# Layer 0 of a two-layer trunk: the matmuls of each small job ranked 40 places ahead, as a group

## The chip, the cores and the metric

The kernel runs on one core of a Trainium2 chip. The metric is the device time of one execution in microseconds, and the median over runs is compared.

## The reference, cut to what matters

The reference computes a trunk of two layers on 512 tokens of width 1024, in fp32. Layer 0 mixes tokens with two recurrences side by side, HGRN2 (4 heads of 128) and RWKV7 (8 heads of 64). Layer 1 does block attention. Each layer has an MLP and a gated side input behind its mixer.

```
def hgrn_rwkv_mixer(h, w_in, w_out, ...):
    u = h @ w_in
    hq, hf, hi, hg, ur = split(u)
    o_a = hgrn2_chunked(silu(hq), 1 - f, hi, log(f))     # f from hf
    o_a = rms_norm(o_a) * silu(hg)
    r, k, v, wd, ad, gd = split(ur + (token_shift(ur) - ur) * mu)
    y = rwkv7_scan(r, decay, k, v, kk, a)                # state per head, token by token
    o_b = (head_layer_norm(y) + bonus) * g
    return concat([o_a, o_b]) @ w_out

for l in range(2):
    x = x + mixer[l](rms_norm(x))
    x = x + square(relu(rms_norm(x) @ w_up[l])) @ w_down[l]
    x = x + rms_norm(p[l] @ ple_proj[l]) * sigmoid(x @ ple_gate[l])
```

## The kernel before

**Large products.** Every product with a weight matrix goes through `gemm`. It splits weights and activations into a high and a low fp32r part and calls `mm3` (L243), three passes of 128x512 for each 128x128 block of weights (L244 whi times high, L245 whi times low, L246 wlo times high). A pass has a weight load of its own. Weights come in halves of 128x512: a DMA on SyncE (L231), a cast on ScalarE (L236, `whi`), a subtraction on VectorE (L237, `wlo`). In layer 0 two raw halves and three split ones are kept. Below, "large pass" means L244 to L246.

**Small jobs.** The recurrences are rewritten in chunks, and their matmuls are small: 64 to 256 columns, most in plain fp32 (two records each in the trace), those of the triangular inverse (L519, L664) in fp16 (one record). Some write only half of the array's columns (L631, L726, L731; the trace has them as 128\*64). They come in groups of three to eight that fill one PSUM tile, and one VectorE or ScalarE instruction then takes the tile away. In the trace the group of `half4` is L664, that of `four` is L519.

**Stages of layer 0.** For each of four heads `step` runs the letters of `ORDER = "AFHBOC"`:
- A: `p2(h, 0)`, the inverse (L519, then L664 level after level, L676 to L690), woven with the side jobs `p3(h-1, 1)` (L707 to L754: states), `p1(h, 1)` (L600 to L631) and `tail(h-1)`.
- F: the three large products f, q, i of the HGRN head (`proj_h`).
- H: `hgrn` (transposes L803, L831, five levels L851, L868 to L884, output transposes L896); its g product is asked for inside.
- B: `proj_rkv(h+1)`, three large products r, k, v of the next RWKV head pair.
- O: `out_piece(h-1)`, the output product of the head before. After the last head `out_piece(3)`.
- C: `p2(h, 1)` woven with `pre(h+1)` and `p3(h, 0)`, then `p1(h+1, 0)`.

**What sets the order.** All instructions are traced in program order; then a planner deals them out. On every engine it takes, among the instructions whose inputs and buffers are ready in its own model of time, the one with the lowest rank. The order on each engine is fixed by this before the chip runs. An instruction's rank is a counter that goes up by one with each traced instruction. `tc.high_priority(offset)` sets the counter back by `offset` at its start, and puts it at its end to where it was at its start. So the instructions inside take no ranks away from what follows, and two such blocks in a row begin at the same rank.

`run` (steps A and C) and the products of step B use an offset of 300:

```
    def run(*gens):
        with tc.high_priority(offset=OFS):
            for g_ in gens:
                for _ in g_:
                    pass
...
                with tc.high_priority(offset=OFS if h else 0):
                    proj(WI[nm, h], evac)
```

The ranks that follow, for the first heads: step A of head 0 has -47 to 105, F and H of head 0 have 253 to 498. Then B (the products r, k and v of head 1) has 199 to 231 three times, step C of head 0 has 199 to 400 with its p1 at 199 to 243, and step A of head 1 has 199 to 427. F and H of head 1 follow with 499 to 744, B for head 2 with 445 to 477, O with 745 to 812, C of head 1 with 513 to 714, and so on. So the large passes of B, and the instructions of C and of the next A, have equal ranks over a good part of their length. Behind the mixer all ranks go up in program order.

PSUM has eight tiles: two for `pj` (large products), two for `pmh` (HGRN and norms), four for `pmr` (RWKV, and the first large products).

Of the kernel before, what the change touches and what calls it, by code (L numbers as in the profile page):

```python
# [34 lines left out]
OFS = 300  # L35
NWARM = 9

P = 128
S = 512
D = 1024  # L40
NJ = S // P
# [144 lines left out]
def trunk(ctx, tc, wts, xT, pT, vecs, lora, cst, lev, seg, rope, gain, out, upto="all", dbg=None, mode=None):  # L186
    nc = tc.nc
    V, A, G, T = nc.vector, nc.scalar, nc.gpsimd, nc.tensor
# [20 lines left out]
    ident = cc("ident")  # L209
# [32 lines left out]

    def mm3(ps, wh, wl, xh, xl, first, last):  # L243
        T.matmul(ps, wh, xh, start=first, stop=False)  # L244
        T.matmul(ps, wh, xl, start=False, stop=False)  # L245
        T.matmul(ps, wl, xh, start=False, stop=last)  # L246
# [37 lines left out]
    class Stats:  # L284
# [4 lines left out]
        def add(self, sq, rhs):  # L289
            for j in range(NJ):  # L290
                T.matmul(self.ps[:, j * self.cols:(j + 1) * self.cols], sq[:, j * P:(j + 1) * P], rhs,
                         start=(self.i == 0 and j == 0), stop=(self.i == self.n - 1),
                         skip_group_check=True)
            self.i += 1
# [31 lines left out]
    def bcast_rows(rt, cols, pool, tag):  # L326
        ps = pool.tile([P, S], F32, name=tag)
        if cols > 1:
            full = nrm.tile([P, S], F32, name="bc")
            V.tensor_copy(full.rearrange("p (c w) -> p c w", w=P // cols),  # L330
                          rt[:, :, None].to_broadcast([P, NJ * cols, P // cols]))
        for j in range(NJ):
            lhs = full[:, j * P:(j + 1) * P] if cols > 1 else rt[:, j:j + 1].to_broadcast([P, P])
            T.transpose(ps[:, j * P:(j + 1) * P], lhs, ident)
        return ps
# [28 lines left out]
    def layer0_mixer(actp):  # L364
# [151 lines left out]
        def four(lhs, rhs):  # L516
            ps = pmr.tile([P, S], F32, name="pmr")
            for i in range(4):
                T.matmul(ps[:, i * P:i * P + P], lhs(i), rhs(i), start=True, stop=True)  # L519
            return ps.rearrange("p (i t) -> p i t", i=4)  # L520
# [67 lines left out]
        def p1(hp, g):  # L588
            lw, bh, kh, ar, rh_, bo, dl, v, y = pre_[hp]
            gs = slice(g * 256, g * 256 + 256)  # L590
            NA, KA, TOK = NAs[g], KAs, []
            un[hp, g] = (NA, TOK)

            for n, (src, dst) in enumerate(((bh, NA), (kh, KA))):
                for h in range(2):
                    A.copy(BH[hs[h], n, :, hs[h]], src[hs[h], gs].rearrange("p (c t) -> p c t", t=64))
                ps = pmr.tile([P, S], F32, name="pmr")
                for c_ in range(4):
                    o = g * 256 + c_ * 64
                    T.matmul(ps[:, c_ * P:c_ * P + P].rearrange("p (x t) -> p x t", x=2), BH[:, n, c_, :],  # L600
                             ar[:, :, o:o + 64], start=True, stop=True)
                pv = ps.rearrange("p (a c x t) -> p a c x t", a=2, c=2, x=2)
                for h in range(2):
                    for c_ in range(2):
                        V.tensor_tensor(dst[hs[c_], :, h, :, hs[c_]], pv[hs[h], :, c_, :, :],
                                        tri[hs[h], None, :, :].to_broadcast([64, 2, 2, 64]), op=OP.mult)
                yield
            for a in range(2):
                j = 2 * g + a
                js = slice(j * P, j * P + P)  # L610

                ps = pmr.tile([P, S], F32, name="pmr")
                for n, src in enumerate((ar[:, 0, :], v, bh, kh)):
                    T.transpose(ps[:, n * P:n * P + P], src[:, js], ident)
                t = E("TOK", 4, [P, 3, P])
                pv = ps.rearrange("p (x f) -> p x f", x=4)
                A.copy(t[:, 0:2, :], pv[:, 0:2, :])
                for c_ in range(2):
                    A.copy(BZ[g][hs[c_], a, :, c_, :], pv[hs[c_], 2:4, :])
                TOK.append(t)  # L620
                yield

            ps = pmr.tile([P, S], F32, name="pmr")
            for i, (a, h) in enumerate(pk):
                T.matmul(ps[:, i * 64:i * 64 + 64], KA[:, a, h, 0, :], TOK[a][:, 1, hs[h]], start=True, stop=True)
# [4 lines left out]
            for i, (a, h) in enumerate(pk):  # L630
                T.matmul(ps[hs[h], a * P:a * P + P], TOK[a][:, 1, hs[h]], KA[:, a, h, 1, :], start=True, stop=True)  # L631
            A.copy(y[:, gs], ps[:, :256])
            yield

        def p2(hp, g):
# [11 lines left out]
            for l in range(1, 6):  # L647
# [12 lines left out]
                def half4(lhs, rhs):  # L660
                    ps = pmr.tile([P, S], F32, name="pmr")
                    pv = ps[:, :256].rearrange("p (i n u) -> p i n u", i=4, u=H)
                    for i in range(4):
                        T.matmul(pv[:, i], lhs[:, i, :], rhs[:, i], start=True, stop=True)  # L664
                    return pv
# [9 lines left out]
            for i, (a, h) in enumerate(pk):  # L675
                T.matmul(ps[:, i * P:i * P + P], NA[:, a, h, 0, :], tt[:, i, :], start=True, stop=False)  # L676
                T.matmul(ps[:, i * P:i * P + P], id16, id16, start=False, stop=True)
# [4 lines left out]
            for i in range(4):  # L682
                T.matmul(ps[:, i * P:i * P + P], er[:, i, :], XT[:, i, :], start=True, stop=False)
                T.matmul(ps[:, i * P:i * P + P], id16, XT[:, i, :], start=False, stop=True)
# [4 lines left out]
            for i, (a, h) in enumerate(pk):  # L689
                T.matmul(ps[:, i * P:i * P + P].rearrange("p (x f) -> p x f", x=2), tt[:, i, :],  # L690
                         TOK[a][:, 0::2, hs[h]], start=True, stop=True)
# [6 lines left out]
        def p3(hp, g):  # L698
# [5 lines left out]
            for a in range(2):  # L704
# [18 lines left out]
            def inner():  # L723
                ps = pmr.tile([P, S], F32, name="pmr")
                for i, (a, h) in enumerate(pk):
                    T.matmul(ps[hs[h], a * P:a * P + P], MU[:, a, 0, hs[h]], NA[:, a, h, 1, :], start=True, stop=True)  # L726
# [3 lines left out]
                for i, (a, h) in enumerate(pk):  # L730
# [21 lines left out]
            for c_ in range(f, 4):  # L752
                ch = 4 * g + c_
                T.matmul(ps[:, c_ * 64:c_ * 64 + 64], SB[:, ch, :], rh_[:, ch * 64:ch * 64 + 64], start=True, stop=True)  # L754
# [43 lines left out]
        def hgrn(h, q, ff, iv, gproj):  # L798
# [3 lines left out]
            for j in range(NJ):  # L802
                T.transpose(ps[:, j * P:j * P + P], iv[:, j * P:j * P + P], ident)  # L803
# [25 lines left out]
            for j in range(NJ):  # L829
                js = slice(j * P, j * P + P)  # L830
                T.matmul(ps[:, js], ks[:, js], d[:, js], start=True, stop=True)  # L831
            V.copy_predicated(at, m8[:, 13, None, :].to_broadcast([P, NJ, P]), j4(ps))
            for l in range(2, 7):
# [15 lines left out]
                for j in range(NJ):  # L849
                    js = slice(j * P, j * P + P)  # L850
                    T.matmul(ps[:, j * 64:j * 64 + 64], ks[:, js], qs[:, j * 64:j * 64 + 64], start=True, stop=True)  # L851
# [15 lines left out]
            for j in range(3):  # L867
                T.transpose(ps[:, j * P:j * P + P], d[:, j * P:j * P + P], ident)  # L868
# [3 lines left out]
            for j in range(3):  # L872
                T.matmul(ps[:, j * P:j * P + P], kt[:, j * P:j * P + P], vt[:, j, :], start=True, stop=True)
# [6 lines left out]
            for j in range(NJ):  # L880
                js = slice(j * P, j * P + P)
                T.matmul(ps[:, js], at[:, j, :], vt[:, j, :], start=True, stop=(j == 0))
                if j:
                    T.matmul(ps[:, js], q[:, js], st_[:, j * P - P:j * P], start=False, stop=True)  # L884
# [10 lines left out]
            for j in range(NJ):  # L895
                T.transpose(ps[:, j * P:j * P + P], ot[:, j * P:j * P + P], ident)  # L896
# [18 lines left out]
        t = {}  # L915
# [431 lines left out]
```

## Time and profile before

| | |
|---|---|
| median of 3 runs | 1511.21 us (1510.91 to 1512.28) |
| the profiled execution | 1511.89 us, span 1510.1 us |
| mean granted TensorE clock | 0.997 |
| TensorE, matmuls | 1478.1 us busy, 98% |
| TensorE, weight loads (overlap the matmuls) | 1191.3 us, 79% |
| VectorE | 937.6 us, 62% |
| ScalarE | 663.1 us, 44% |
| GpSimd | 138.4 us, 9% |
| the mixer of layer 0 | 0 to 454 us |

The start of a matmul is recorded, its end is modelled, and neighbours overlap in the records: a pass of 128x512 shows some 0.39 us although the next one starts 0.23 us later. What a pass costs is therefore read from start to start. The profile's rows merge instructions of one line that follow each other; a count (x4) tells how many records they are.

### The profile page before, as it was taken

The page shows a single profiled execution, that of the slowest core. Times are in us where ns is not written, and L with a number is a line of the kernel's source. Part 1 is how long each engine was busy: PE and PEld are TensorE (multiplying, and loading weights), DVE is VectorE, ACT ScalarE, POOL GpSimd, SP SyncE. Part 2 cuts the span into 40 slices and gives each one's busy share as a digit, 9 for nine tenths or more (in the row PEclk, how much of TensorE's full clock was granted, in tenths as well). Part 3 has the DMA queues.
Part 4 walks back from the last instruction along what each step waited for, and adds up shares of the span by engine and source line. Part 5 has one row for each costly group of instructions (what it writes and reads, how often), then busy time and mean ns, then how long its engine had stood idle before and what let it go on. Part 6 is the DMA issues. An engine that isn't in the chain of part 4 may idle for free.

```text
span 1510.1 us, 20495 instructions
## 1 busy us (share of the span) xinstructions
PE 1478.1 (98%) x7546; PEld 1191.3 (79%) x7546; DVE 937.6 (62%) x1835; ACT 663.1 (44%) x1269; POOL 138.4 (9%) x133
## 2 busy tenths in 40 slices
PE   8899999999989999999999999999999999999998
PEld 6678777777667888888888888777778888888887
DVE  6878797687785664444446648377575444445463
ACT  4675545554446433333334534455634333333342
POOL 4121220310205000000000200000220000000000
PEclk9999999999999999999999999999999999999999
DMA  5110111211123233333333432221123333333331
GB/s 179 56 36 22 55 50 39 66 29 47 39 91 106 90 98 98 98 98 98 98 95 98 124 118 84 77 63 50 56 80 95 95 101 98 98 96 93 98 98 70
DMA packets 67109, 123.88 MB, mean 82 GB/s; under 512 B 7632, under 2 KB 8016, under 8 KB 67008
## 3 DMA queue, kind: packets, MB, share of 16 engines
q1 hardware_dynamic: 65376, 118.57, 25.6%
q10 hardware_dynamic: 1152, 2.43, 0.5%
q0 software_dynamic: 480, 1.57, 0.3%
q8 instruction: 59, 0.97, 0.3%
q14 instruction: 42, 0.34, 0.1%
HBM read 120.45 MB, written 2.10 MB: 81 GB/s over the span
## 4 chain that ended last, share of the span: by engine, by line
PE 87%; DVE 7%; ACT 3%; issue 2%; DMA 1%; POOL 1%; SPq 0%; DVEq 0%; ACTq 0%; POOLq 0%
PE pj L244 20%; PE pj L246 20%; PE pj L245 20%; PE pmr L1273 1%; PE pmr L245 1%; PE pmr L1249 1%; PE pmr L246 1%; PE pmr L244 1%; PE pj L1176 1%; PE pmr L1176 1%; PE pj L1178 1%; PE pmr L1177 1%; PE pmr L1178 1%; PE pj L1177 1%; PE pmh L1176 1%
## 5 line engine op out<-in xcount | busy, mean ns | idle before, releaser
L236 ACT CAST whi<-wr 128x512 fp32r<-128x512 f32 x428 | 265.0, 621 | 549.2 <-PE pj L245 421.9
L237 DVE TENSOR_TENSOR wlo<-wr,whi 128x512 fp32r<-128x512 f32 x428 | 312.5, 733 | 197.6 <-ACT whi L236 193.6
L244 PE MATMUL pj<-act,whi 128*128 128x512 f32 (+1 forms) x856 | 338.1, 396 | 1.2 <-DVE h L935 1.0
L245 PE MATMUL pj<-act,whi 128*128 128x512 f32 (+1 forms) x856 | 336.8, 394 | 0.0
L246 PE MATMUL pj<-act,wlo 128*128 128x512 f32 (+1 forms) x856 | 335.7, 393 | 0.5 <-DVE wlo L237 0.5
L244 PE MATMUL pj<-hid,whi 128*128 128x512 f32 x512 | 199.2, 389 | 0.0
L245 PE MATMUL pj<-hid,whi 128*128 128x512 f32 x512 | 199.2, 389 | 0.0
L246 PE MATMUL pj<-hid,wlo 128*128 128x512 f32 x512 | 199.2, 389 | 0.0
L244 PEld LDWEIGHTS pj<-act,whi 128*128 128x128 f32 x856 | 161.1, 188 | 34.4 <-ACT k L491 1.4
L246 PEld LDWEIGHTS pj<-act,wlo 128*128 128x128 f32 x856 | 161.2, 188 | 32.5 <-DVE wlo L237 1.5
L245 PEld LDWEIGHTS pj<-act,whi 128*128 128x128 f32 x856 | 161.2, 188 | 31.1 <-issue 1.5
L1115 DVE TENSOR_TENSOR x<-x,pj 128x512 f32<-128x512 f32 x128 | 88.0, 688 | 80.6 <-PE pj L246 80.2
L245 PEld LDWEIGHTS pj<-hid,whi 128*128 128x128 f32 x512 | 96.1, 188 | 20.0
L244 PEld LDWEIGHTS pj<-hid,whi 128*128 128x128 f32 x512 | 96.1, 188 | 19.9
L246 PEld LDWEIGHTS pj<-hid,wlo 128*128 128x128 f32 x512 | 96.1, 188 | 19.9
L319 POOL TENSOR_TENSOR acc<-acc,xsq 128x512 f32<-128x512 f32 x35 | 48.7, 1393 | 628.8 <-ACT xsq L313 616.0
L1104 DVE SCALAR_TENSOR_TENSOR r<-pj,rb 128x512 f32<-128x512 f32 x56 | 38.7, 691 | 84.0 <-PE pj L246 84.0
L278 DVE TENSOR_TENSOR hid<-r,hid 128x512 fp32r<-128x512 f32 x64 | 44.3, 691 | 41.5 <-ACT hid L277 41.4
L1105 ACT ACTIVATE r<-r 128x512 f32<-128x512 f32 x64 | 40.5, 632 | 21.6 <-DVE r L1104 21.5
L277 ACT CAST hid<-r 128x512 fp32r<-128x512 f32 x64 | 39.8, 621 | 1.9
L280 ACT ACTIVATE act<-x,vec 128x512 fp32r<-128x512 f32 x32 | 22.9, 720 | 29.4 <-DVE x L1133 12.7
L244 PE MATMUL pj<-os,whi 128*128 128x512 f32 x64 | 28.3, 445 | 4.4 <-DVE x L946 2.8
(387 smaller groups left out, 2225.8 us busy)
## 6 DMA issues: line engine op xcount, KB each, us to landing
wr<-in_wts_dram SPq DMA_DIRECT2D x428, 256.0 KB, 2.7
x<-in_xT_dram SPq DMA_DIRECT2D x8, 256.0 KB, 6.3
sr<-in_wts_dram SPq DMA_DIRECT2D x8, 256.0 KB, 5.3
out_dram<-x SPq DMA_DIRECT2D x7, 256.0 KB, 2.0
r<-in_pT_dram ACTq DMA_DIRECT2D x4, 256.0 KB, 3.0
lw<-in_lora_dram POOLq DMA_DIRECT2D x4, 192.0 KB, 3.1
tq<-in_rope_dram ACTq DMA_DIRECT2D x1, 512.0 KB, 6.7
tk<-in_rope_dram ACTq DMA_DIRECT2D x1, 512.0 KB, 7.6
```

The costliest lines, as they stand in the source:

```text
L236: A.copy(hi, raw)
L237: V.tensor_sub(lo, raw, hi.bitcast(F32))
L244: T.matmul(ps, wh, xh, start=first, stop=False)
L245: T.matmul(ps, wh, xl, start=False, stop=False)
L246: T.matmul(ps, wl, xh, start=False, stop=last)
L277: A.copy(h, src)
L278: V.tensor_sub(l, src, h.bitcast(F32))
L319: G.tensor_add(self.t, self.t, sq)
L1104: V.scalar_tensor_tensor(r, q, 0.0, nf[0], op0=OP.max, op1=OP.mult)
L1105: A.activation(r, r, AF.Square)
L1115: V.tensor_add(x[k], x[k], ps)
L1176: T.matmul(ps[j], xh, wh, start=k == 0, stop=False)
```

## The change

A context manager `tight` is added, and the matmuls of nearly every small job are put into it, each group in one block: `Stats.add` (L291), `bcast_rows` (L334), `four` (L519), in `p1` L600, L614, L625 and L631, in `p2` L664, L676 with L677, L683 with L684, and L690, in `p3` L710 with L711, L726, L731 and L754, in `hgrn` L803, L831, L851, L868, L873, L882 with L884, and L896. Nothing is computed otherwise, and the instructions, tiles and buffers are the same. Left outside are L531, L548, L579, L764, L780 (single matmuls of 512 columns), L707 and L744. `Stats.add` and `bcast_rows` serve the norms of both layers. Nested in `run`, the block counts from the rank that the step has reached, less 40. The sites look alike, so three stand for all:

```
+TIGHT = 40
...
+    def tight():
+
+        return tc.high_priority(offset=TIGHT)
...
                 def half4(lhs, rhs):
                     ps = pmr.tile([P, S], F32, name="pmr")
                     pv = ps[:, :256].rearrange("p (i n u) -> p i n u", i=4, u=H)
-                    for i in range(4):
-                        T.matmul(pv[:, i], lhs[:, i, :], rhs[:, i], start=True, stop=True)
+                    with tight():
+                        for i in range(4):
+                            T.matmul(pv[:, i], lhs[:, i, :], rhs[:, i], start=True, stop=True)
                     return pv
...
                 T.matmul(ps[:, :256], MU[:, a, 0, :], bz[:, 0].rearrange("p c f -> p (c f)"), start=True, stop=True)
-                for c_ in range(2):
-                    o = ps[:, 256 + c_ * P:256 + c_ * P + P]
-                    T.matmul(o, bz[:, 0, c_, :], MU[:, a, 1, :], start=True, stop=False)
-                    T.matmul(o, bz[:, 1, c_, :], TOK[a][:, 1, :], start=False, stop=True)
+                with tight():
+                    for c_ in range(2):
+                        o = ps[:, 256 + c_ * P:256 + c_ * P + P]
+                        T.matmul(o, bz[:, 0, c_, :], MU[:, a, 1, :], start=True, stop=False)
+                        T.matmul(o, bz[:, 1, c_, :], TOK[a][:, 1, :], start=False, stop=True)
...
                 ps = pmr.tile([P, S], F32, name="pmr")
-                for i, (a, h) in enumerate(pk):
-                    T.matmul(ps[hs[h], a * P:a * P + P], MU[:, a, 1, hs[h]], NA[:, a, h, 1, :], start=True, stop=True)
+                with tight():
+                    for i, (a, h) in enumerate(pk):
+                        T.matmul(ps[hs[h], a * P:a * P + P], MU[:, a, 1, hs[h]], NA[:, a, h, 1, :], start=True, stop=True)
                 V.tensor_add(y[:, gs], y[:, gs], ps[:, :256])
```

## Rows read from the trace of the kernel before

**Rows 1.** The page: busy us by engine, share of the span, instructions.

```profile
PE 1478.1 (98%) x7546; PEld 1191.3 (79%) x7546; DVE 937.6 (62%) x1835; ACT 663.1 (44%) x1269; POOL 138.4 (9%) x133
```

**Rows 2.** Stretches of the span: length, busy us (and instructions) by engine, granted clock, DMA.

```profile
33.00:389.00 356.00, 344.27 (x2396) 269.75 (x2395) 275.17 (x652) 192.09 (x431) 64.34 (x68) 1.00 0.15 45
389.00:454.00 65.00, 57.45 (x339) 44.67 (x339) 54.48 (x120) 32.34 (x64) 11.10 (x10) 0.97 0.22 65
475.00:1088.00 613.00, 612.46 (x2764) 495.85 (x2763) 350.66 (x655) 257.33 (x478) 23.74 (x18) 1.00 0.29 90
```

**Rows 3.** What TensorE waited for, 33 to 454 us: us, times, longest.

```profile
PE pj L244 <- DVE x L946: 2.8, 4, 1.3
...
PE pmr L664 <- ACT PP L667: 1.5, 2, 0.7
...
PE pj L246 <- DVE wlo L237: 0.5, 2, 0.2
...
PE pmr L707 <- ACT MU L693: 0.3, 1, 0.3
```

**Rows 4.** TensorE in order of time, 162.8 to 165 us: start, length, line, tiles, shape.

```profile
162.78 0.39 PE L710 MATMUL pmr<-MU,BZ 128*128 128x128 f32 x2
...
163.45 0.39 PE L711 MATMUL pmr<-TOK,BZ 128*128 128x128 f32 x2
...
163.91 0.40 PE L245 MATMUL pj<-act,whi 128*128 128x512 f32 x1
...
164.84 0.39 PE L246 MATMUL pj<-act,wlo 128*128 128x512 f32 x1
```

**Rows 5.** TensorE in order of time, 165.3 to 166.4 us, an L664 group.

```profile
165.31 0.20 PE L664 MATMUL pmr<-PP,XT 128*128 128x64 f16 x1
165.35 0.48 PE L245 MATMUL pj<-act,whi 128*128 128x512 f32 x1
...
166.38 0.20 PE L664 MATMUL pmr<-PP,XT 128*128 128x64 f16 x1
```

**Rows 6.** TensorE in order of time, 108.3 to 108.6 us, two L664 groups.

```profile
108.31 0.29 PE L664 MATMUL pmr<-PP,XT 128*128 128x64 f16 x4
...
108.57 0.67 PE L548 MATMUL pmr<-lwa,lw 128*128 128x512 f32 x1
```

**Rows 7.** TensorE in order of time, 381.6 to 382.4 us, an L731 group.

```profile
381.61 0.43 PE L731 MATMUL pmr<-NA,MU 128*64 128x128 f32 x2
381.97 0.50 PE L244 MATMUL pj<-act,whi 128*128 128x512 f32 x1
382.40 0.43 PE L731 MATMUL pmr<-NA,MU 128*64 128x128 f32 x2
```

**Rows 8.** TensorE in order of time, 415.7 to 416.4 us, another L731 group.

```profile
415.72 0.66 PE L731 MATMUL pmr<-NA,MU 128*64 128x128 f32 x8
416.31 0.49 PE L873 MATMUL pmh<-vt,h 128*128 128x128 f32 x2
```

**Rows 9.** TensorE in order of time, 169.3 to 170.7 us, L710 and L711.

```profile
169.29 0.38 PE L710 MATMUL pmr<-MU,BZ 128*128 128x128 f32 x2
...
170.66 0.38 PE L711 MATMUL pmr<-TOK,BZ 128*128 128x128 f32 x2
```

**Rows 10.** The chain of waits, 389 to 439 us: start, length, what.

```profile
389.74 0.45 PE pmh L803 x4
...
428.12 0.69 DVE e L781
...
430.08 0.68 DVE h L893
...
438.14 0.72 PE pj L244 x2
```

**Rows 11.** Stretches around the last wait of layer 0's mixer (columns as rows 2).

```profile
434.00:438.00 4.00, 2.48 (x11) 1.68 (x9) 3.50 (x6) 1.68 (x4) 1.28 (x1) 1.00 0.64 197
438.00:443.00 5.00, 4.86 (x12) 3.27 (x12) 2.97 (x5) 1.13 (x3) 0.00 (x0) 0.66 0.49 159
```

More of the change, by code (lines that the diff above doesn't have):

```diff
@@ L289, in add @@
         def add(self, sq, rhs):
[L290 to L293, printed above, removed]
+            with tight():
+                for j in range(NJ):
+                    T.matmul(self.ps[:, j * self.cols:(j + 1) * self.cols], sq[:, j * P:(j + 1) * P], rhs,
+                             start=(self.i == 0 and j == 0), stop=(self.i == self.n - 1),
+                             skip_group_check=True)
             self.i += 1
@@ L597, in p1 @@
                 ps = pmr.tile([P, S], F32, name="pmr")
[L598 to L601, printed above, removed]
+                with tight():
+                    for c_ in range(4):
+                        o = g * 256 + c_ * 64
+                        T.matmul(ps[:, c_ * P:c_ * P + P].rearrange("p (x t) -> p x t", x=2), BH[:, n, c_, :],
+                                 ar[:, :, o:o + 64], start=True, stop=True)
                 pv = ps.rearrange("p (a c x t) -> p a c x t", a=2, c=2, x=2)
@@ L629, in p1 @@
             ps = pmr.tile([P, S], F32, name="pmr")
[L630 to L631 removed]
+            with tight():
+                for i, (a, h) in enumerate(pk):
+                    T.matmul(ps[hs[h], a * P:a * P + P], TOK[a][:, 1, hs[h]], KA[:, a, h, 1, :], start=True, stop=True)
             A.copy(y[:, gs], ps[:, :256])
@@ L751, in p3 @@
             f = 1 if g == 0 else 0
-            for c_ in range(f, 4):
-                ch = 4 * g + c_
-                T.matmul(ps[:, c_ * 64:c_ * 64 + 64], SB[:, ch, :], rh_[:, ch * 64:ch * 64 + 64], start=True, stop=True)
+            with tight():
+                for c_ in range(f, 4):
+                    ch = 4 * g + c_
+                    T.matmul(ps[:, c_ * 64:c_ * 64 + 64], SB[:, ch, :], rh_[:, ch * 64:ch * 64 + 64], start=True, stop=True)
             yg = y[:, g * 256 + f * 64:g * 256 + 256]
@@ L828, in hgrn @@
             ps = pmh.tile([P, S], F32, name="pmh")
-            for j in range(NJ):
-                js = slice(j * P, j * P + P)
-                T.matmul(ps[:, js], ks[:, js], d[:, js], start=True, stop=True)
+            with tight():
+                for j in range(NJ):
+                    js = slice(j * P, j * P + P)
+                    T.matmul(ps[:, js], ks[:, js], d[:, js], start=True, stop=True)
             V.copy_predicated(at, m8[:, 13, None, :].to_broadcast([P, NJ, P]), j4(ps))
@@ L848, in hgrn @@
                 ps = pmh.tile([P, S], F32, name="pmh")
-                for j in range(NJ):
-                    js = slice(j * P, j * P + P)
-                    T.matmul(ps[:, j * 64:j * 64 + 64], ks[:, js], qs[:, j * 64:j * 64 + 64], start=True, stop=True)
+                with tight():
+                    for j in range(NJ):
+                        js = slice(j * P, j * P + P)
+                        T.matmul(ps[:, j * 64:j * 64 + 64], ks[:, js], qs[:, j * 64:j * 64 + 64], start=True, stop=True)
                 def hi(t):
@@ L871, in hgrn @@
             ps = pmh.tile([P, S], F32, name="pmh")
-            for j in range(3):
-                T.matmul(ps[:, j * P:j * P + P], kt[:, j * P:j * P + P], vt[:, j, :], start=True, stop=True)
+            with tight():
+                for j in range(3):
+                    T.matmul(ps[:, j * P:j * P + P], kt[:, j * P:j * P + P], vt[:, j, :], start=True, stop=True)
             st_ = Hh()
@@ L879, in hgrn @@
             ps = pmh.tile([P, S], F32, name="pmh")
[L880 to L884, printed above, removed]
+            with tight():
+                for j in range(NJ):
+                    js = slice(j * P, j * P + P)
+                    T.matmul(ps[:, js], at[:, j, :], vt[:, j, :], start=True, stop=(j == 0))
+                    if j:
+                        T.matmul(ps[:, js], q[:, js], st_[:, j * P - P:j * P], start=False, stop=True)
             sq = Hh()
```

64 lines of the change are left out of this document (38 added, 26 removed).

## The prediction

> **What bounds the kernel now.** I read the page first, then the table of stretches, then the list of what TensorE waited for, and last the order of single passes in time.
> TensorE is busy 98% of the span, the next engine 62% [rows 1]. So a time can come out lower only where TensorE does its work in less time, or where its few gaps close.
> The table of stretches says where [rows 2]: in the mixer of layer 0, 33 to 454 us, TensorE is busy 344.27 + 57.45 = 401.72 of 421 us, so 19.3 us are gaps, 7.5 of them in the last 65 us. From 475 to 1088 us it stands still for 0.5 us. The change can matter in the first 454 us and hardly later.
> The wait list of that stretch has 17 kinds of wait, the longest 2.8 us in total over four times [rows 3]: the engine is not held by one thing, it is full.
>
> What is it full of? A large pass (128x512) takes its place every 0.23 us when large follows large: five starts from 163.91 to 164.84 [rows 4]. The small jobs come as groups of four to eight. Some groups run together, some are cut, with one large pass after every small one [rows 5, 7]. The cut groups are what the change is about.
>
> **Part 1: the cuts that go.** Price first, by three kinds of small job.
> - *fp16, 64 columns (L664).* Cut: the four small passes of a group, a large one behind each, start from 165.31 to 166.38, so one small and one large pass take 0.357 us together [rows 5]. Uncut: two groups of four start at 108.31 and the job behind them at 108.57, 0.13 us for four, 0.03 each [rows 6]. A cut costs 0.357 - 0.23 - 0.03 = 0.10 us.
> - *fp16, 128 columns (L519).* An estimate from the same rows: the cut step is taken as the same 0.357, and 64 columns more cost 64/512 x 0.23 = 0.03 us in an uncut group [rows 4], so a pass there is 0.06. A cut costs 0.357 - 0.23 - 0.06 = 0.07 us.
> - *Half-width fp32 (L731, 128\*64).* Cut: from 381.61 to 382.40, 0.79 a step of one small matmul and one large pass, four such steps [rows 7]. Uncut: the whole group from 415.72 to the next job at 416.31 takes 0.59 us [rows 8]. Four steps cut are 4 x 0.79 = 3.16; uncut they are 0.59 + 0.43 (a large pass behind such a matmul, 381.97 to 382.40, rows 7) + 3 x 0.23 = 1.71. The group of four saves 1.4 us.
> - *fp32, full width (L710, L711).* Cut: three steps from 169.29 to 170.66, 0.457 each [rows 9]. Uncut: three from 162.78 to 163.45, 0.223 each [rows 4]. A cut costs 0.457 - 0.223 - 0.23 = 0.00. These cuts are free; so I hold those of L625, L803 and L851, also fp32.
>
> How many: in order of time TensorE has 31 places where a single large pass stands inside an L664 group (7 near 165 to 172 us, 10 near 264 to 276, 14 near 375 to 388; rows 5 are the first group), 6 inside L519 groups (261 and 365 us), and 3 inside one L731 group (rows 7). Sum: 31 x 0.10 + 6 x 0.07 + 1.4 = 3.1 + 0.4 + 1.4 = 4.9 us of TensorE's time.
>
> Why they would go: in the plan before, the passes of proj_rkv and the instructions of steps C and A begin at one and the same rank (199 for head 1), so the planner deals them out in turns, one small, one large. With the group 40 ranks lower and itself without ranks of its own, all four lie below the large pass that now ties with the second of them. All cuts by a single pass inside a group whose parts are ready together should close. Where the parts become ready one by one (L851 near 188 and 292 us, with ten large passes between, of which the first waits for VectorE's wlo) they stay, and cost nothing.
>
> Here a page speaks against the change. In [rows 9] a large pass between two full-width fp32 jobs costs nothing beyond itself. The Trainium skill, "TensorE: Matmul & The Clock Gate", section "Step-by-step: what each phase is for", says that TensorE loads the next pass's weights while the present one still runs; by it every cut would be covered like this, and the sum of this part would be 0. The trace agrees for fp32 and does not for fp16, where the step is 0.10 us longer than its parts [rows 5, 6]. The sum goes by the rows; that the cover wins is rival 1.
>
> **Part 2: groups jump forward by 40 ranks and take none.** This moves more than the cuts. Job p2 has 108 ranked instructions, 84 of them now in such blocks; step C of head 0 has 202, of which 111; hgrn has 45. Since a block takes no ranks, whatever follows it in the same step moves up: the 202 ranks of step C become 91, and the same VectorE and ScalarE instructions stand further ahead of the weight casts of proj_rkv and of hgrn. No instruction is added and no DMA is moved by itself; the weight loads on SyncE follow the casts that free their buffers. What it may cost: a VectorE job of 512 columns is some 0.7 us (L781, rows 10), and TensorE waited 0.5 us for wlo in the whole mixer [rows 3]. Three split half blocks of weights stand between the casts and TensorE; if this cover broke once at each of the four heads by one such job, it would be 4 x 0.7 = 2.8 us. What it may bring: a cut group of four ends three large passes and cuts later than an uncut one, 3 x 0.33 = 1.0 us; some ten L664 groups were cut, so the RWKV chain gains up to 10 us of lead on its own side work. That is worth time only where TensorE stood waiting for it, the gaps that the wait list puts to PP, BZ, tt, X and MU, from 1.5 down to 0.3 us [rows 3], together 5.1 us at most. Between +2.8 and -5.1 I take 0: of the waits that set the two ends, the one for wlo is 0.5 us today, and the five others end on ScalarE and VectorE steps that the change does not shorten.
>
> **Part 3: does the saving reach the end?** TensorE is full up to 389 us, so what it saves before comes out there (all 40 cuts lie before 389). Behind it the last stage is a chain: hgrn of head 3 starts with its transposes at 389.74; its output is scaled on VectorE at 430.08, behind the end of the RWKV tail (428.12); and the last output product waits until 438.14 [rows 10]. This stage moves as a whole by what hgrn starts earlier. Against that, the side groups that now pass ahead of the last f, q and i passes push these back, each by its 0.13 to 0.6 us [rows 6, 8]; I count three at the lower price and take 0.4 off. Behind that wait the granted clock of 438 to 443 us is 0.66, so 1.2 GHz for some 3.4 of the 5 us, after TensorE had been busy 2.48 of the 4 us before [rows 11]. Half of 3.4 us is lost by it. If the wait (4 - 2.48 = 1.5 us) went and the clock held, 1.5 + 1.7 = 3.2 us would be gained; if both doubled, as much would be lost. I take 0, since the order at this place (tail, then hgrn, then the last weights) is made by steps that the change leaves in their order. The norms of the other layers (L291, L334) move 40 ranks too; but TensorE stands still for 0.5 us in the 613 us of the MLP and its norm [rows 2], and I count nothing.
>
> **Sum.** -4.9 + 0 + 0.4 = -4.5 us. The profiled execution takes 1511.89 us, span 1510.1 and 1.8 around it; it would be 1507.4. The median of the runs is 0.7 us lower, 1511.21, so the forecast is 1506.7 us.
>
> **Rivals.**
> 1. *Little or nothing is left.* Either the large pass covers the small one's start everywhere, as it does for fp32 [rows 9]: the sum is 0 + 0.4 and the time 1511.6, chance 0.06, since rows 5 and 6 speak against it. Or the plan keeps half of the cuts, because the parts of a group become ready one after another: -2.5 + 0.4 = -2.1 us, 1509.1, chance 0.12. Or the last stage gives it back, its gaps of 7.5 us [rows 2] growing by what was saved: 1510 to 1512, chance 0.10.
> 2. *Slower: hgrn of the last head is put behind.* The RWKV side's VectorE work now ranks ahead of hgrn's, and hgrn, not the RWKV tail, ends the mixer. Place: 389 to 438 us, VectorE busy 54.48 of 65 us there [rows 2]. Price: some 0.7 us for each job like L781 that goes ahead of a step of hgrn's chain [rows 10]. It decides from the seventh such job on (7 x 0.7 = 4.9, which eats the 4.5); with twelve it is 8.4 - 4.5 = +3.9 us, 1515.1. For it: one such job already stands ahead of hgrn's last steps there, and VectorE (54.48 us) is nearly as busy as TensorE (57.45 us) in this stage [rows 2]. Against: hgrn's own groups get the 40 ranks too, and a RWKV chain that is done sooner leaves VectorE sooner.
> 3. *More than the cuts:* the lead of part 2 closes the 5.1 us of gaps, 1511.2 - 4.5 - 5.1 = 1501.6 at the most; half of it gives 1504.1.
>
> **Chances.** A measurement of this kernel can tell about 0.2%, 3 us, from no change. The forecast's own case (all cuts go, the rest within 1.5 us) 0.43, rival 3 0.12, rival 1 in its three forms 0.28, rival 2 0.17. Faster by over 0.2% (below 1508.2): 0.43 and 0.12, of which a little may fall above: 0.54. Within 0.2%: rival 1 and a start of rival 2: 0.29. Slower than 1514.2: 0.17. The range reaches from half of rival 3's extra to the point where rival 2 has just become visible: 1502.5 to 1514.0. The likeliest case alone is 1505.0 to 1508.2.
>
> **What would show it.** Right: L664, L519 and L731 as groups of x4 and x8 without a large pass between them, at the cut places; TensorE busy in 33 to 454 us about 397 us and the mixer ending near 449 us with its gaps still near 19 us. Part 2 wrong: a longer wait for wlo, or for hgrn's h and KS tiles, in the wait list. Rival 2: hgrn's last scaling (L893) coming later behind its first transposes (L803) than the 430.08 - 389.74 = 40.3 us of now [rows 10]. The prediction fails if the gaps of the mixer change by more than 3 us either way, or if the cuts stay.

## The result: 1535.4 us, slower by 1.6%

The changed kernel takes 1535.4 us (median of four runs, 1534.11 to 1538.29) against 1511.06 us of the kernel before: a ratio of 1.0163, 95% interval [1.0145, 1.018]. The forecast was 1506.7 us with a range up to 1514.0. The sign was wrong, and the time lies outside the range.

The profiled execution takes 1538.29 us with a span of 1536.5, so 26.4 us more than before. Where they lie is read from three landmarks. The last pass of layer 0's output product ends at 452.9 us before and at 473.3 after: 20.4 us are lost in the mixer of layer 0. The last instruction of TensorE comes another 6.0 us later, and that is in the norms behind the mixer.

First the page of the changed kernel, the row that answers [rows 1]:

```profile
PE 1492.5 (97%) x7546; PEld 1206.4 (79%) x7546; DVE 935.3 (61%) x1835; ACT 664.4 (43%) x1269; POOL 138.1 (9%) x133
```

The number of instructions is the same and TensorE is busy 14.4 us longer: the same passes take more time. The table of stretches of the kernel before, from 33 us to its mixer's end (columns as in rows 2):

```profile
33.00:452.90 419.90, 400.62 (x2728) 313.54 (x2728) 328.56 (x769) 223.34 (x492) 75.35 (x77) 1.00 0.16 49
```

The same table of the changed kernel: the whole mixer, four stretches of its end, and the MLP, which answers the last row of [rows 2]:

```profile
33.00:473.30 440.30, 415.25 (x2729) 328.25 (x2728) 325.64 (x756) 223.80 (x491) 74.81 (x77) 0.98 0.15 46
...
410.00:420.00 10.00, 9.99 (x49) 7.33 (x48) 7.28 (x22) 5.64 (x9) 0.00 (x0) 1.00 0.22 62
420.00:430.00 10.00, 6.28 (x37) 5.03 (x35) 7.59 (x13) 6.12 (x13) 6.27 (x6) 1.00 0.24 69
430.00:440.00 10.00, 9.26 (x41) 8.18 (x39) 6.66 (x13) 2.17 (x6) 3.13 (x3) 0.57 0.00 0
440.00:450.00 10.00, 7.78 (x32) 6.50 (x32) 5.80 (x16) 4.22 (x8) 0.00 (x0) 0.75 0.43 136
...
485.00:1098.00 613.00, 611.72 (x2756) 495.73 (x2757) 352.31 (x668) 253.38 (x469) 18.89 (x14) 1.00 0.30 92
```

TensorE's busy time in the mixer grows by 415.25 - 400.62 = 14.6 us and its gaps from 19.3 to 25.1 us, by 5.8. The granted clock is 0.57 and 0.75 in 430 to 450 us, so TensorE runs at 1.2 GHz for more than half of these 20 us; before, it was at full speed but for the few us of [rows 11]. One line shows it pass by pass: these six passes (L873 there) have a median of 275 ns in the kernel before. The three numbers in ns are the shortest, the median and the longest.

```profile
L898 PE MATMUL pmh<-vt,h x6: 421/422/580, 440.3 to 441.5; 128*128 128x128 f32 x6
```

Now the order of single passes. This is the changed kernel, TensorE from 383.6 us (the lines L664, L726 and L731 of before are L677, L744 and L750 here):

```profile
383.62 0.40 PE L249 MATMUL pj<-act,whi 128*128 128x512 f32 x1
383.94 0.44 PE L744 MATMUL pmr<-NA,MU 128*64 128x128 f32 x4
384.31 0.20 PE L677 MATMUL pmr<-X,n 128*128 128x64 f16 x1
384.45 0.43 PE L744 MATMUL pmr<-NA,MU 128*64 128x128 f32 x2
384.81 0.20 PE L677 MATMUL pmr<-X,n 128*128 128x64 f16 x1
384.94 0.43 PE L744 MATMUL pmr<-NA,MU 128*64 128x128 f32 x2
385.31 0.23 PE L677 MATMUL pmr<-X,n 128*128 128x64 f16 x2
385.38 0.47 PE L763 MATMUL pmr<-SB,GB 128*128 128x128 f32 x2
```

No large pass stands inside a group of these three lines any more, as forecast. But two small groups, the half-width L744 and the fp16 L677, are now dealt out in turns: 1.44 us from 383.94 to 385.38 for eight half-width records and four fp16 ones. Run as whole groups they take 0.59 + 0.13 = 0.72 us [rows 6, 8]. In place of the cuts by large passes stand cuts by other small jobs, and many more of them. In the order of TensorE's instructions, the small groups of layer 0 are cut at 78 places by large passes and at 42 by other small jobs in the kernel before; in the changed kernel at 29 and 332.

The three half-width lines by shape show the price (line, shapes, count, busy us and mean ns). Before:

```profile
L631 PE MATMUL pmr<-KA,TOK 128*64 128x128 f32 x64 | 7.6, 291 | 0.0
L731 PE MATMUL pmr<-NA,MU 128*64 128x128 f32 x64 | 6.3, 287 | 0.0
L726 PE MATMUL pmr<-NA,MU 128*64 128x128 f32 x64 | 5.3, 285 | 0.0
```

After:

```profile
L750 PE MATMUL pmr<-NA,MU 128*64 128x128 f32 x64 | 11.1, 297 | 0.0
L643 PE MATMUL pmr<-KA,TOK 128*64 128x128 f32 x64 | 9.6, 295 | 0.0
L744 PE MATMUL pmr<-NA,MU 128*64 128x128 f32 x64 | 9.1, 293 | 0.0
```

A pass has nearly the same mean length (288 and 295 ns), yet the lines occupy 29.8 us in place of 19.2: alone, a pass no longer overlaps the next of its kind (above, four records of L744 take 0.44 us and two take 0.43). These 10.6 us count time twice where other passes overlap. From the end of one pass to the end of the next, which counts nothing twice, the half-width passes take 25.3 us in place of 16.8: 8.5 of the 14.6 us by which TensorE's busy time in the mixer grows.

The start of hgrn in head 3, its four transposes (duration min/median/max, first and last start), and its last transposes; before, the two stand at 389.6 and 431.0:

```profile
L824 PE MATMUL pmh<-cs,h x4: 273/273/328, 416.0 to 417.7; 128*128 128x128 f32 x4
...
L923 PE MATMUL pmh<-cs,h x4: 271/272/272, 454.1 to 454.4; 128*128 128x128 f32 x4
```

So hgrn of head 3, hgrn(3) below, starts 26 us later. The RWKV side is earlier instead: the last VectorE job of its tail (L801, L781 in the kernel before) starts at 419.2 us, where it started at 428.1. Last, what TensorE waited for behind the mixer (us in total, times, longest), before and after:

```profile
PE pmh L291 <- POOL acc L319: 0.8, 1, 0.8
```

```profile
PE pmh L297 <- POOL acc L325: 7.2, 3, 3.7
```

Three one-column norm matmuls now stand in TensorE's queue ahead of work that is ready, and wait for POOL's sum: 6.4 us more, which answers for the 6.0 us behind the mixer.

### The profile page after: what moved, and what is told of

The parts are those of the page before. It is cut to its first block, busy times and chain, and to the rows that moved or that the text cites. A ratio compares the mean times of both kernels' runs of the same rounds, so it can differ in the third digit from the quotient of the medians.

```text
span 1536.5 us, 20498 instructions
## 1 busy us (share of the span) xinstructions
PE 1492.5 (97%) x7546; PEld 1206.4 (79%) x7546; DVE 935.3 (61%) x1835; ACT 664.4 (43%) x1269; POOL 138.1 (9%) x133
## 4 chain that ended last, share of the span: by engine, by line
PE 66%; DVE 2%; POOL 1%; ACT 1%; issue 1%; POOLq 0%; ACTq 0%; DVEq 0%
PE pj L249 17%; PE pj L250 17%; PE pj L251 17%; PE pmr L1300 1%; PE pmr L1276 1%; PE pj L1203 1%; PE pj L1205 1%; PE pj L1204 1%; PE pmh L1203 1%; PE pmh L1205 1%; PE pmh L1204 1%; PE pmr L1205 1%; PE pmr L1203 1%; PE pmr L1204 1%; PE pmr L249 1%; PE pmr L251 1%
## 5 line engine op out<-in xcount | busy, mean ns | idle before, releaser
L251 PE MATMUL pj<-hid,wlo 128*128 128x512 f32 x512 | 199.6, 390 | 0.0
L250 PE MATMUL pj<-hid,whi 128*128 128x512 f32 x512 | 199.6, 390 | 0.0
```

## The experiments

The question was which of four things carries the loss: the jump of 40 ranks, the fact that a block takes no ranks, the late hgrn(3), or the norms. In all versions "ranks given back" is this block, with which a group jumps as in the change while what follows keeps the ranks that it had:

```
@contextmanager
def tight():
    p = tc.cur_priority
    with tc.high_priority(offset=TIGHT):
        yield
        n = tc.cur_priority - (p - TIGHT)
    tc.cur_priority = p + n
```

All results in one table. "Cuts" are places inside the small groups of layer 0 at which at least one large pass stands / only other small jobs stand, in the order of TensorE's instructions; "hgrn(3)" is the number of the matmul with which it starts. From the profile: the end of the mixer, and the low clock, the sum of length x (1 - granted clock) over stretches of 10 us from 33 us to that end. The ratio is to the kernel before, run on the same chip.

| version | us | ratio [95%] | cuts | hgrn(3) | mixer's end | low clock |
|---|---|---|---|---|---|---|
| before | 1511.1 | 1 | 78/42 | 2002 | 452.9 | 1.7 |
| after | 1535.4 | 1.0163 [1.0145, 1.018] | 29/332 | 2087 | 473.3 | 8.5 |
| keep40 | 1513.27 | 1.0018 [1.0008, 1.0027] | 33/34 | 2002 | 449.4 | 1.7 |
| keep40n | 1507.55 | 0.9977 [0.9967, 0.9987] | 20/36 | 2002 | 446.5 | 0 |
| free0 | 1535.62 | 1.0172 [1.0151, 1.0193] | 34/359 | 2087 | 476.9 | 6.8 |
| nonorm | 1536.76 | 1.0169 [1.0155, 1.0183] | 17/333 | 2087 | 477.8 | 11.9 |
| onlynorm | 1515.73 | 1.0032 [1.0021, 1.0044] | 85/39 | 2002 | 449.1 | 0 |
| onlycut | 1508.39 | 0.999 [0.9981, 0.9998] | 36/65 | 2002 | 449.6 | 1.7 |
| onlycutfree | 1524.82 | 1.0103 [1.0084, 1.0121] | 41/199 | 2051 | 472.5 | 15.4 |
| few_alt | 1527.82 | 1.0103 [1.0089, 1.0116] | 46/208 | 1993 | 469.7 | 11.9 |
| heldf16 | 1529.34 | 1.0121 [1.0106, 1.0136] | 19/123 | 2087 | 472.8 | 10.2 |
| heldhalf | 1529.2 | 1.0117 [1.0099, 1.0134] | 17/303 | 2087 | 473.5 | 13.7 |
| after_r120 | 1533.21 | 1.0153 [1.0138, 1.0168] | 32/330 | 1973 | 465.1 | 8.5 |
| late_only | 1513.1 | 1.0014 [1.0003, 1.0024] | 22/28 | 2087 | 453.7 | 3.4 |
| alt_only | 1530.96 | 1.0125 [1.0105, 1.0144] | 19/345 | 1983 | 472.1 | 8.5 |
| keep160n | 1514.16 | 1.0024 [1.0012, 1.0036] | 23/26 | 2002 | 454.6 | 6.8 |
| keepn_r120 | 1516.13 | 1.0032 [1.0021, 1.0043] | 22/34 | 1954 | 457.1 | 3.4 |

**keep40 and free0: the jump, or the ranks?** keep40 is the change with ranks given back; free0 is the change with a jump of 0, so that a block only leaves its ranks out.

```
-    def tight(): return tc.high_priority(offset=40)
+    def tight(): ...        # keep40: ranks given back
+    TIGHT = 0               # free0
```

> The jump of 40 stays, but each block gives back the ranks of its instructions to the count, so that what follows it stands behind it as before. Theory A (the blocks take no ranks, so neighbouring small groups tie with each other and alternate on TensorE, fp16 with half-width and fp32): the alternation goes, the mixer of layer 0 loses its 20 us, the norms behind it still wait some 5 us: 1511 - 4.9 + 5 = 1511 us, between 1507 and 1515. Theory B (the jump of 40 itself puts the jobs into a worse order): nothing of the jump is gone, so 1528 us or more.

> The blocks stay and take no ranks, but the jump is 0. Theory A: the alternation of small groups stays, the norms are no longer ahead: 1535 - 5 = 1530 us, between 1524 and 1536. Theory B: the order is nearly that of before, 1508 to 1515 us.

keep40 comes to 1.0018, free0 to 1.0172, as slow as the change itself; both lie in the ranges of theory A. So the loss is not the jump: it is that blocks take no ranks. What follows in a step then moves up against everything else, and the groups of neighbouring steps come to lie on the same ranks.

**nonorm, onlynorm, keep40n: the norms.** nonorm is the change without blocks round the norms of one column; onlynorm is the kernel before with blocks round these alone; keep40n is keep40 without them.

```
-            with tight():
+            with tight() if self.cols > 1 else ExitStack():
```

> As the changed kernel, without the block around the four matmuls of the one-column norms (Stats.add and bcast_rows with cols 1); those of the RWKV statistics keep it. Theory C (the norm's matmuls now stand in TensorE's queue before GpSimd's acc is done, and the large passes behind them wait: 7.2 us of waits for acc against 0.8 before): about 6 us less, 1529.5 us, between 1527.5 and 1531.5. Rival: the wait only hides another wait behind it, 1533 to 1536 us.

> The kernel before, with the block (jump 40, no ranks taken) around the matmuls of the one-column norms alone. Theory C (these matmuls come into TensorE's queue before GpSimd has finished acc, at the end of the mixer and at the two norms of layer 1, and the large passes behind them wait): waits for acc of some 7.2 us instead of 0.8, and 1510.9 + 5.8 = 1516.7 us, between 1514.5 and 1519. Rival (the 5.7 us between the two kernels with ranks given back came from another order in the mixer): 1509 to 1513 us.

> Jump of 40, ranks given back, one-column norms without the block. Theories A and C together: the 4.9 us of cuts by large passes that the prediction summed up are saved and nothing is lost: 1506.5 us, between 1503 and 1510. Theory B: 1523 us or more.

onlynorm costs 0.32% (4.8 us), and keep40 against keep40n 0.41% (6.2 us). The wait list of onlynorm behind the mixer has the 6.4 us of the changed kernel. In its profile the mixer ends 3.7 us earlier than before (1.7 of them are low clock that before had), and from there to TensorE's last instruction it takes 7.6 us longer:

```profile
PE pmh L297 <- POOL acc L325: 7.2, 3, 3.7
```

nonorm was a miss: this wait goes back to 0.7 us, but the mixer's end moves from 473.3 to 477.8 us, and the time doesn't improve. free0, where the norms don't jump either, is alike: a wait of 0.8 us, the mixer's end at 476.9. Where no ranks are taken, the jump of the norms gives about as much in layer 0 as it costs later. Why stays open. In the profiles the first hgrn starts at 71.5 us with these blocks and at 80.8 without, but keep40 and keep40n differ in the same way (72.6 and 79.1), and there the mixer with the blocks ends later.

keep40n is what the change was meant to be, and it is faster than before, by 0.23%. Its page, mixer, half-width lines and the same kind of place as above:

```profile
PE 1470.4 (98%) x7546; PEld 1192.1 (79%) x7546; DVE 936.6 (62%) x1835; ACT 663.0 (44%) x1269; POOL 139.3 (9%) x133
```

```profile
33.00:446.50 413.50, 392.06 (x2724) 313.58 (x2723) 326.87 (x767) 223.29 (x492) 75.90 (x77) 1.00 0.17 49
```

```profile
L647 PE MATMUL pmr<-KA,TOK 128*64 128x128 f32 x64 | 7.0, 288 | 0.0
L754 PE MATMUL pmr<-NA,MU 128*64 128x128 f32 x64 | 5.3, 285 | 0.0
L748 PE MATMUL pmr<-NA,MU 128*64 128x128 f32 x64 | 5.3, 284 | 0.0
```

```profile
373.46 0.28 PE L681 MATMUL pmr<-PP,XT 128*128 128x64 f16 x4
373.58 0.28 PE L681 MATMUL pmr<-XT,PP 128*128 128x64 f16 x4
373.79 0.66 PE L748 MATMUL pmr<-NA,MU 128*64 128x128 f32 x8
374.38 0.50 PE L255 MATMUL pj<-act,wlo 128*128 128x512 f32 x1
```

Eight fp16 and eight half-width records take 0.92 us here; alternated, the changed kernel needed 1.44 for twelve.

**onlycut and onlycutfree: the cuts alone.** Blocks only round L519, L664 and L731, the three groups of part 1, with ranks given back and without.

> The kernel before, with the block around the three kinds of group alone that the prediction priced (L519, L664, L731), jump 40, ranks given back. If the saving is that of the cuts by large passes: TensorE's large passes in the mixer some 4 to 5 us shorter, 1510.9 - 4.9 = 1506 us, between 1503.5 and 1508.5. If the other groups' jump made the saving in the kernel with all groups: 1509 to 1513 us.

> Blocks round L519, L664 and L731 alone (jump 40), and these take no ranks; it differs from the version of 1508.39 us, whose blocks give their ranks back, in that alone. In the plan, other small jobs cut a small group 199 times against 65, and hgrn(3) starts at matmul 2051 against 2002. Theory D (taking no ranks makes neighbouring groups alternate and hgrn(3) late): alternation costs (199 - 65) x 13.6 us / 290 = 6.3 us by the changed kernel's price, lateness 49/85 of 11 us = 6.3, so 1508.4 + 6 to 13 = 1515 to 1521. Rival, that it is the number of jobs that jump and not the ranks that they leave out: 1508.4 with 1.5 us either way.

onlycut gains 0.1%, [0.0002, 0.0019]: the cuts are worth something, less than forecast. Its large passes are shorter by what was expected, 199.5 us end to end in the mixer against 203.7 before, at the same low clock, but 65 cuts by small jobs stand against 42, and its half-width passes take 17.8 us against 16.8. Without the ranks given back, the same three blocks cost 1.1% more, and that was more than expected.

**heldf16 and heldhalf: a part of the groups.** nonorm, with ranks given back by the fp16 groups alone, or by the half-width groups alone.

> The changed kernel without the block around the one-column norms, and the fp16 groups (half4, four) give their ranks back; all others take none. In the plan the cuts of small groups by other small jobs are 123, against 42 before and 333 with nothing given back. Theory A by the count of cuts (17 us of TensorE for 290 cuts more, 0.06 us each): 1510.9 - 4.9 + 81 x 0.06 = 1510.9 us, between 1506 and 1517. Theory A2 (only the switches between half-width and full-width passes cost, and p1 and inner are still cut 59 times): 1516 to 1526 us.

> The changed kernel without the block around the one-column norms, and only the half-width groups (L631, L726, L731 of the kernel before) give their ranks back. 303 cuts by small jobs are left in the plan. Theory A by the count: nearly all stays lost, 1510.9 - 4.9 + 261 x 0.06 = 1521.7 us or more, up to 1536. Theory A2: half-width groups stand mostly together, so their 8.5 us come back: 1536.8 - 8.5 = 1528 us, and by the time of the half-width passes in the trace near 17 us instead of 25.

Each wins back 0.5% (1.0169 to 1.0121 and 1.0117). heldf16 lies above the ranges of both theories; heldhalf lies in theory A's range and near theory A2's 1528 us and so can't tell them apart, and its half-width passes take 21.5 us end to end (25.3 in nonorm), where theory A2 had near 17. heldf16 removes 210 of the cuts by small jobs and gains no more than heldhalf, which removes 30. So one price per cut doesn't describe this. That it counts what kind of pass is cut by what would fit, but no run here shows it by itself.

**after_r120 and keepn_r120: hgrn(3) earlier.** The change, and keep40n, with two steps of head 3 raised by 120 ranks (given back):

```
 elif c == "F":
+    with ahead(120 if h == 3 else 0):
         for nm in "fqi": proj_h(nm, h)
 elif c == "H":
+    with ahead(120 if h == 3 else 0):
         hgrn(h, ...)
```

> The changed kernel with one addition: the f, q, i products and hgrn of head 3 get their ranks 120 places lower, and the ranks are given back to what follows. In the plan hgrn(3) then starts at TensorE's matmul 1973 (before the change 2002, changed 2087), while the small groups stay as much alternated with each other as in the changed kernel (330 such cuts against 332). Theory D: of the 20 us that layer 0's mixer lost, the part that comes from a late hgrn(3) is +5.8 us of gaps and +5.1 us of low clock; it should come back: 1535.4 - 9 to 11 = about 1525 us (1521 to 1530), hgrn(3) beginning before 400 us. Rival, that the switching between small jobs carries the whole loss: 1532 us or more.

> The version of 1507.55 us with f, q, i and hgrn of head 3 raised by 120 ranks (ranks given back), as a control of that raise where hgrn(3) isn't late: it starts at matmul 1954 in place of 2002. Theory D: the raise by itself gives little, 1507.5 with 3 us either way, so a gain of 9 to 11 us in the changed kernel is the lateness and not the raise. Rival, that an earlier hgrn(3) is worth something in any plan (last stage's gaps of 7.5 us before the change): 1502 or less.

Both missed; after_r120 comes out on its rival's side. There hgrn(3) does start earlier, at 396.7 us, and the mixer's end comes 8.2 us earlier, but the median falls by 2.2 us alone, within both intervals; the low clock stays, 8.5 us. And keepn_r120 loses 8.6 us against keep40n: an hgrn(3) that is too early makes the RWKV tail late (its last matmuls start at 438.8 us in place of 421.9). So this place has an optimum, and the raise is no clean test.

**late_only, alt_only, few_alt: one at a time.** These separate the two. late_only is keep40n with the same two steps put back by 60 ranks: hgrn(3) as late as in the changed kernel, groups whole. alt_only is nonorm with the two steps raised by 100: hgrn(3) as before the change, groups alternated. few_alt is onlycutfree with a raise of 40.

> The version of 1507.55 us (ranks given back, no blocks round the one-column norms), with f, q, i and hgrn of head 3 put 60 ranks back. In the plan hgrn(3) then starts at TensorE's matmul 2087 and the RWKV tail stands at 2107, as in the changed kernel (2087 and 2094; before 2002 and 2170), but small groups are cut as rarely as there (22 times by a large pass, 28 by another small job). So it is the lateness alone. Theory D (lateness is worth the difference of the mixer's ends without low clock between the changed kernel and the one with hgrn(3) raised, 464.8 - 456.6 = 8 us, and some 3 to 5 us of low clock with it): 1515 to 1520. Rival, that alternation carries the loss and lateness nothing: 1507.5 with 2 us either way.

> The version of 1536.76 us (the change without blocks round the one-column norms; no ranks taken), with f, q, i and hgrn of head 3 raised by 100 ranks: hgrn(3) starts at matmul 1983, the tail stands at 2170 and hgrn's last transposes at 2183, as before the change (2002, 2170, 2183), while small jobs cut small groups 345 times (20 to 42 before and in the version of 1507.55 us). So it is the alternation alone. Theory D: 1507.5 + 10 to 12 us of switches between kinds of pass + 3 to 7 us of low clock = 1521 to 1527. Rival, that lateness carries most of the loss: 1512 or less. Rival, that the two don't add up and alternation alone has it all: 1532 or more.

> The version of 1524.82 us (blocks round L519, L664 and L731 alone, no ranks taken), with f, q, i and hgrn of head 3 raised by 40 ranks: hgrn(3) starts at matmul 1993 (2051 without the raise, 2002 before), small jobs cut small groups 208 times (199 without the raise, 65 with ranks given back). Theory D: the half lateness (49 of 85 places) goes, 58% of 8 us = 4.7 and 1 to 3 us of low clock with it: 1517 to 1519.5. Rival, that what is left out of the ranks costs by alternation alone: 1523 to 1526.

With keep40n and nonorm they make a square:

| ratio to before | hgrn(3) as before | hgrn(3) late |
|---|---|---|
| groups whole | 0.9977 [0.9967, 0.9987] | 1.0014 [1.0003, 1.0024] |
| groups alternated | 1.0125 [1.0105, 1.0144] | 1.0169 [1.0155, 1.0183] |

Lateness costs 0.0037 or 0.0044 (5.6 or 6.6 us), alternation 0.0148 or 0.0155 (22 or 23 us): the two add up, and alternation is three to four times the larger. Each of the three missed what theory D had for it: late_only and alt_only lie between theory D and a rival, few_alt above both. My 11 us for lateness were nearly twice too much, and what I gave to alternation was too little. few_alt shows no gain at all: without its half lateness onlycutfree stays at 1.0103, where the square would give some 0.002 for it, about what these two intervals leave open.

Where the 22 us lie is seen in alt_only against keep40n, its mixer and its half-width lines:

```profile
33.00:472.10 439.10, 413.87 (x2725) 326.28 (x2724) 327.60 (x768) 224.22 (x492) 75.55 (x77) 0.98 0.15 46
```

```profile
L759 PE MATMUL pmr<-NA,MU 128*64 128x128 f32 x64 | 11.2, 301 | 0.0
L753 PE MATMUL pmr<-NA,MU 128*64 128x128 f32 x64 | 9.8, 303 | 0.0
L652 PE MATMUL pmr<-KA,TOK 128*64 128x128 f32 x64 | 9.7, 298 | 0.0
```

The mixer is 25.6 us longer: 21.8 us more of busy TensorE, 3.8 of gaps. From the end of one pass to the end of the next, added up by kind, the half-width passes have 10.7 us more, full-width fp32 ones of up to 256 columns 6.0, fp16 3.2, the fp32 ones of 512 columns 1.3 and the large ones 0.5. The low clock (8.5 us by the table) lies within these terms, and its share of each I can't separate. The mean clock of each single run bounds it: at 0.994 alt_only took 1526.54 us and keep40n 1510.07, one run each, on chips whose kernels before differ by 1 us; so some 15 of the 22 us stay at an equal clock.

**keep160n: a larger jump.** keep40n with TIGHT = 160.

> The version of 1507.55 us (every group but the one-column norms' in a block, ranks given back), with a jump of 160 places in place of 40. In the plan 23 large passes and 26 small jobs cut a small group (20 and 36 with 40), and hgrn(3) starts at 2002 as before. Theory D (what counts is the ranks taken, not the size of the jump): 1507.5, from 1505 to 1510. Rival, that a jump of more places disturbs the order of the work (groups of later steps ahead of large passes that others wait for): 1512 or more.

1514.16 us, the rival's side: 6.6 us slower than with 40. The cuts are as few and hgrn(3) starts at the same place. In the profile the mixer is 8.1 us longer than that of keep40n: 3.9 us more of busy TensorE and 4.2 of gaps. The low clock is 6.8 us, but it is not the whole of the loss: two runs with a mean clock of 0.995 took 1513.38 and 1513.9 us, and the one of keep40n with that clock 1507.53. What makes the gaps stays open. Its mixer, and its longest stretch of low clock:

```profile
33.00:454.60 421.60, 395.99 (x2723) 320.33 (x2722) 328.58 (x764) 222.97 (x492) 73.40 (x77) 0.98 0.16 48
...
406.00:418.00 12.00, 11.96 (x62) 11.07 (x63) 6.19 (x13) 3.46 (x9) 2.43 (x2) 0.57 0.01 1
```

## Why the prediction was wrong

**Part 1, the cuts: the mechanism right, the size near.** L664, L519 and L731 lie without large passes between them in the changed kernel (40 such cuts counted before, none after). Forecast were 4.9 us of TensorE's time; end to end the large passes of the mixer take 203.7 us before and 198.2 in keep40n; up to 1.7 of these 5.5 us is the clock that before lost at 438 to 443 us [rows 11]. As a time, keep40n gives 3.5 us (0.0023, from 0.0013 to 0.0033) where 4.5 were forecast, and the three groups alone (onlycut) 1.5 us. The change itself keeps them: its large passes take 199.6 us, and that gain lies inside its loss.

**Part 2, "take none", cost at 0: the step that failed.** I named that whatever follows a block moves up, and asked what this does to weight casts on VectorE and to gaps, between +2.8 and -5.1 us. Both ends were about waits. I did not ask what the groups do to each other: when a group's own ranks vanish, the next group starts on them, and two independent small jobs tie just as the small job and the large pass had tied before. The rows to price it stood in front of me. A half-width matmul with something else behind it took 0.43 us and a whole group of eight 0.59 [rows 7, 8]; I used these for cuts by large passes alone. Entered 65 times in alt_only and 28 times in keep40n, the half-width sections account for 10.7 of the 25.6 us that alternation adds to the mixer. The Trainium skill, "TensorEngine Tiling (Array Packing)", section "Key Properties", states that a change of the tiling mode drains TensorE; the trace agrees in so far as such a change takes time, and does not show whether it is a drain. In the mixer of the kernel before, from end to end, a half-width pass takes 0.25 us behind a full-width one, fp16 or fp32 alike, and 0.05 on average behind its own kind; an fp16 pass takes a median of 0.135 us behind a half-width one, 0.055 behind a full-width fp32 one of 128 columns and 0.029 behind its own kind. Full-width passes pay too where the type changes: an fp32 one of 128 columns takes 0.165 behind an fp16 one, 0.112 behind its own kind.

**Rival 2: the place right, the mechanism not.** "hgrn of the last head is put behind" did happen, by 26 us in the profile, but not through VectorE jobs. Each RWKV step lost about half its ranks, so the whole RWKV chain of head 3 moved ahead of the f, q, i passes and hgrn. The mark I had set did not trip for that reason: L893 (now L919) starts at 453.2 us, 37.2 behind the first transposes at 416.0, where it was 40.3. The RWKV tail that had run beside it is over earlier, so hgrn(3) is late as a whole, and the last stage has less beside it: TensorE is busy 6.28 of 10 us at 420 us. The square prices it at 5.6 to 6.6 us, where rival 2 had 8.4 for twelve jobs.

**Part 3, the saving reaches the end: right where there is one.** keep40n's mixer ends 6.3 us earlier in the profile (446.53 against 452.87) and TensorE's last instruction 6.4. That I counted nothing for the norms was wrong by 5 to 6 us in onlynorm and keep40. I argued from TensorE's idle time of before, 0.5 us, but a jump doesn't fill idle time here: it puts a matmul whose input is not there at the head of an in-order queue.

**The clock, taken as 0 with 3.2 us either way.** It was part of it, though no experiment sets it: 8.5 us at the most in the changed kernel against 1.7. By the two runs of equal clock above it is the smaller part of what alternation costs.

**The marks.** I had written that the forecast fails if the mixer's gaps change by more than 3 us; they grew by 5.8. TensorE was to be busy some 397 us up to an end near 449; it is busy 415.25 up to 473.3. keep40n, with 392.06 up to 446.5 and gaps of 21.4 us, comes near to what the forecast described; its profiled execution is the fastest of its eight, 1505.54 us.

## What to carry to other kernels

A rank offset and the ranks a block uses up are two edits: give the ranks back, or everything behind the block moves too, and independent small jobs of equal rank are dealt out in turns. Price a cut by what cuts it. A step of one half-width matmul and one fp16 pass took 0.50 us here (384.31 to 384.81), of which whole groups need 0.59 / 4 + 0.03 = 0.18 [rows 6, 8]; so alternating costs 0.32 us a step, where an fp16 pass cut off by a large one cost 0.10. And a matmul should only be moved ahead of others if its operand is ready there, since the queue behind it waits.

## What the hardware showed that was not expected

The low clock comes and goes with plans that differ little. keep160n is at 0.57 for the 12 us from 406 us. The stretch before that and the one in which it falls:

```profile
390.00:400.00 10.00, 9.11 (x75) 6.87 (x72) 9.34 (x18) 8.90 (x16) 2.49 (x2) 1.00 0.19 61
400.00:410.00 10.00, 8.95 (x64) 7.87 (x62) 9.86 (x17) 4.67 (x12) 7.30 (x6) 0.84 0.10 28
```

The granted clock of keep40n is 1.00 up to the end of its mixer, though in the same stretches TensorE is busy less:

```profile
390.00:400.00 10.00, 8.23 (x62) 6.48 (x60) 9.85 (x16) 6.15 (x15) 7.06 (x6) 1.00 0.18 57
400.00:410.00 10.00, 8.79 (x71) 7.75 (x72) 6.90 (x17) 4.24 (x12) 2.37 (x2) 1.00 0.01 2
```

What makes it fall in the one and not in the other stays open; the busy share of these rows does not order them. It also makes times scatter: onlycutfree's runs reach from 1523.13 to 1532.49 us, and the profiled one, with 15.4 us of low clock, is the slowest of them. The mixer's ends and the low clock in the table are those of single executions, so the ratios carry the verdicts.
